# Two-layer attention and retention trunk: products of constants ahead of the first tokens, and a new order of the first loads and steps

## The chip, the core and the metric

The kernel runs on one core of a Trainium2 chip. A core has five engines, each with its own queue of instructions that it works through in order: TensorE (PE, matrix products and transposes; PEld is its loading of the stationary operand), VectorE (DVE), ScalarE (ACT), GpSimd (POOL) and SyncE (SP), which here only issues transfers. The transfers themselves are carried out by 16 DMA engines. The metric is the device time of one execution in microseconds (us); lower is better.

## The reference

The input is one sequence of 2048 tokens with 1024 features. Each of two layers normalises the tokens, projects them to eight sections of 512 columns, runs chunked softmax attention on one half of the heads and chunkwise retention on the other, gates both and adds the output projection:

```python
def hybrid_layer(x, norm_gain, w_in, w_out, rel_bias, cos, sin):
    hn = rms_norm(x, norm_gain)
    proj = hn @ w_in.astype(hn.dtype)
    aq, ak, av, ag, rq, rk, rv, rg = jnp.split(proj, cuts, axis=-1)
    ya = chunked_rel_attention(aq, ak, av, rel_bias)
    yr = chunkwise_retention(rq, rk, rv, cos, sin)
    y = jnp.concatenate([ya * jax.nn.silu(ag), yr * jax.nn.silu(rg)], axis=-1)
    return x + y @ w_out.astype(x.dtype)
```

The tables cos and sin come from the integer positions, times a fixed list of inverse frequencies. The result is normalised once more. All arithmetic of the reference is float32.

## The kernel before

Every float32 operand of a large product is split into an upper half (float16) and a lower half (the float16 rest), and a product is three products of halves: upper by upper, upper by lower, lower by upper. So a weight section passes through five steps before PE can use it: its squares are summed (ACT, L1346), the sum is cast (DVE, L1350) and added over the partitions by a product with ones (PE, L1356), a power-of-two scale is made of it by five small steps (DVE, L1363 to L1367), the upper half is written (ACT, L1426) and then the lower half (DVE, L1429). A token tile of 128 tokens has its own chain: squares (ACT, L249), root (DVE L210, POOL L212), scaling by root and gain (DVE, L256), eight transposes for each tile in the first group (PE, L265), upper half (ACT, L274) and lower half (DVE, L283).

The sweep goes over two layers, four weight groups s and four token groups n of 512 tokens (four tiles each). Before the first group can be multiplied, its four token tiles x0 to x3, four weight sections W0 to W3 (for q, k and the retention's q and k) and then four sections V0 to V3 have to be loaded and converted; tiles x4 to x7 of the next token group are loaded behind them. The first group's products come in this order on PE: sections 0 and 1 token tile by token tile (L722, 24 products of 128 columns for each pair of section and tile), sections 2 and 3 for all 512 tokens at once (L740, 24 products of 512 columns each), then the products with V (dense_V, L760, four tiles of 24 products). From then on PE has the work of all later groups.

The order of work on all engines is written out by hand. All first loads are issued on SP in one list (L1397, before any step). Then `do` runs a string of step names, and each step appends its instructions to the queues of the engines that it uses. The names that matter here:

- `xsq3 xrs3 xmul3 xtr3 xhi3 xlo3`: squares, root, scaling, transposes, upper and lower half of token tile 3; `xdma` is the transfer that transposes the halves of tiles 4 and up (SP, L236 and L237).
- `Wsq2 Wlp2 Wsc2 Whi2 Wlo2`: squares, cast, scale, upper and lower half of weight section 2; `V` for the V sections. W2 and W3, V0 and V1, V2 and V3 share their cast and scale.
- `g`: the next of three steps of the gain's own scale (DVE and PE, L165 to L189). Its input is the small load `gs`. `gb` is the load of the gain rows for all partitions, which `xmul` reads.
- `t`: the next step of the rotary tables (L89 to L125): the first in the string is the product of positions and inverse frequencies (ACT, L99, loads `pos` and `inv`), then come small reductions on DVE (L93 to L115) and sines on ACT. `u` is the same for two later groups.
- `r`: the relative bias (load `rl`): six transposes and a copy (L541, L542), then twelve products and two copies (L547, L548). `bs` and `bt` build bias tiles of it.
- `d`: the next part of the first group's products: eight parts of 24 products (L722), two evacuations, then three parts of eight (L740) and an evacuation for each of the sections 2 and 3.
- `Tu`, `Vu`: small scales that follow from the sections' scales; `Tu` also scales the retention's mask (load `msk`).

After the string, the generator dense_V and the dense products of the three following groups run in parts of eight products. With each part one pair of `ring["listed"]` is taken: the first of its two strings runs ahead of that part's attention work and the second behind it. This list of 96 pairs holds the steps of tiles 4 to 15 and those of the next weight group (`T` and `U` names).

`ms0` is a tile of 1024 float32 columns in PSUM; each weight scale uses two columns of its lower half. `ones` is a column of ones in bfloat16, set by POOL at the start and broadcast to a 128x128 operand.

Of the kernel before, what the change touches and what calls it, by code (L numbers as in the profile page):

```python
# [18 lines left out]
P = 128  # L19
# [8 lines left out]
def hybrid_trunk(ctx: ExitStack, tc: tile.TileContext, x, pos, gain, gcol, w_in, w_out, rel, fgain,  # L28
# [8 lines left out]
    act, dve, pool, pe, sp = nc.scalar, nc.vector, nc.gpsimd, nc.tensor, nc.sync  # L37
# [20 lines left out]
    ones = cp.tile([P, 1], BF16, tag="ones", name="ones")  # L58
# [24 lines left out]
    def tables(ns, wk):  # L83

        ang, k, r, k2 = wk
        pi = k2.bitcast(I32)
        for i, n in enumerate(ns):
            src = pos[n * 512:(n + 1) * 512].rearrange("(h c) -> h c", h=2)[None].to_broadcast([64, 2, 256])
            sp.dma_start(pi[:, i * 256:(i + 1) * 256], src)  # L89
        yield  # L90

        def mulsub(dst, kk, c):
            dve.scalar_tensor_tensor(out=dst, in0=kk, scalar=-c, in1=dst, op0=ALU.mult, op1=ALU.add)  # L93

        def rnd(dst, src, mul):
            dve.tensor_scalar(dst, src, mul, MAGIC, op0=ALU.mult, op1=ALU.add)
            dve.tensor_scalar(dst, dst, -MAGIC, None, op0=ALU.add)

        act.activation(ang, pi, AF.Copy, scale=invf_sb[:, 0:1])  # L99
        yield  # L100
        rnd(k, ang, 1.0 / P1)
        yield
        for c in (PA, PB, PC):
            mulsub(ang, k, c)
            yield
        dve.scalar_tensor_tensor(out=k2, in0=k, scalar=-(PD + PE_), in1=ang, op0=ALU.mult, op1=ALU.add)
        yield
        rnd(k2, k2, 1.0 / TWO_PI)
        yield
        for kk, c in ((k2, QA), (k, PD), (k2, QB), (k, PE_), (k2, QC)):  # L110
            mulsub(ang, kk, c)
            yield
        dve.tensor_scalar(ang, ang, PI_CL, -PI_CL, op0=ALU.min, op1=ALU.max)
        yield
        dve.scalar_tensor_tensor(out=k, in0=ang, scalar=-1.0, in1=ang, op0=ALU.mult, op1=ALU.max)  # L115
        yield
        act.activation(r, ang, AF.Sin)
        act.activation(k2, k, AF.Sin, scale=-1.0, bias=quarter[:, 0:1])
        yield
        act.activation(ang, r, AF.Copy, scale=-1.0)  # L120
        yield
        def store(i, n):
            for part, src in enumerate((k2, k2, ang, r)):
                rows = tab_d[n][part // 2, part % 2 * 64:part % 2 * 64 + 64].rearrange("f (h c) -> (f h) c", h=2)
                sp.dma_start(rows, src[:, i * 256:(i + 1) * 256])  # L125
            tab_done.add(n)

        store(0, ns[0])
        if len(ns) > 1:
            later(7, lambda: store(1, ns[1]))  # L130
        yield
# [69 lines left out]
    ring = {}  # L201
# [325 lines left out]
    def rel_reverse():  # L527

        c8 = (RELW + 1) // P
        rl = b2.tile([P, D], F32, tag="q", name="rl")  # L530
        rt = b1.tile([P, c8, NH], F32, tag="dT", name="rt")
        anti = b1.tile([P, KT, P], F16, tag="ktok", name="anti").rearrange("p k c -> p (k c)").bitcast(F32)[:, 0:P]
        pool.memset(rl[0:NH, 0:RELW + 1], 0.0)
        pool.memset(anti, 0.0)
        pool.affine_select(out=anti, in_=anti, compare_op=ALU.not_equal, fill=1.0, base=1 - P, pattern=[[1, P]],
                           channel_multiplier=1)
        sp.dma_start(rl[0:NH, 0:RELW], rel)
        yield
        ps = psR.tile([P, c8, NH], F32, tag="small", name="rlt")
        for c in range(c8):  # L540
            pe.transpose(ps[:, c, :], rl[0:NH, c * P:(c + 1) * P], ident[0:NH, 0:NH])  # L541
        dve.tensor_copy(rt, ps)  # L542
        yield
        for hf in range(2):
            pr = psR.tile([P, c8 // 2, P], F32, tag="small", name=f"rlr{hf}")
            for c in range(c8 // 2):
                pe.matmul(pr[0:NH, c, :], rt[:, c8 - 1 - hf * c8 // 2 - c, :], anti, start=True, stop=True)  # L547
            dve.tensor_copy(rl[0:NH, hf * P * c8 // 2:(hf + 1) * P * c8 // 2],  # L548
                            pr[0:NH].rearrange("p c i -> p (c i)"))
        sp.dma_start(rel_d, rl[0:NH, 0:RELW + 1])  # L550
        yield
# [45 lines left out]
    def later(k, fn):  # L597
        deferred.append([k, fn])
# [734 lines left out]
    def go_on(*gens):  # L1333
        for g_ in gens:
            next(g_, None)
# [40 lines left out]
    t0 = tables((0,), [gp.tile([P, 256], F32, tag="gt", name=f"wk{i}") for i in range(4)])  # L1376
    rl_ = rel_reverse()
# [15 lines left out]
    for j in range(4):  # L1393
        loads[f"V{j}"] = lambda j=j: v_in(j)
        if j < 3:
            loads[f"W{j}"] = lambda j=j: W.load(j)
    for nm in "x0 gs msk W0 gb x1 inv pos x2 W1 x3 rl W2 W3 dc V0 V1 V2 V3 x4 x5 x6 x7".split():  # L1397
        loads[nm]()
    gs = gain_scale(0)
    ms0 = psS.tile([P, D], F32, tag="S", name="ms0")  # L1400
    spare = [h_.rearrange("p k c -> p (k c)")[:, i * 2 * D:(i + 1) * 2 * D] for h_ in far[1] for i in range(2)]
    xk = [Tok(t, xs0[t], None) if t < 4 else Tok(t, late[t - 4], spare[t - 4]) for t in range(8)]
    d0 = dense_T(0, 0, 0, g00, st0)
# [37 lines left out]
    def V_un():  # L1441
        if not vu:
            vu.append(V_units(0, 0, g00, scs["V0"].i + scs["V2"].i, "V0_0"))
        next(vu[0])

    t1 = tables((1, 2), [xs0[1 + i // 2][:, i % 2 * 512:(i % 2 + 1) * 512] for i in range(4)])
    x8 = (sp.dma_start(late[t - 8], x[t * P:(t + 1) * P, :]) for t in range(8, 12))
    steps = {"x8": lambda: go_on(x8), "d": lambda: go_on(d0), "t": lambda: go_on(t0), "u": lambda: go_on(t1), "r": lambda: go_on(rl_), "g": lambda: go_on(gs),
             "Tu": T_un, "Vu": V_un, "bs": lambda: go_on(bs0), "bt": lambda: go_on(bt0)}
    for t in range(8):  # L1450
        for f in ("sq", "rs", "mul", "tr", "hi", "lo", "dma"):
# [7 lines left out]
    def do(names):  # L1459
        for nm in names.split():  # L1460
            steps[nm]()

    do("g xsq0 xrs0 Wsq0 xsq1 g Wlp0 g Wsc0 xmul0 Whi0 xtr0 xsq2 t xrs1 xhi0 xmul1 Wsq1 Wlo0 xrs2 t xtr1 xlo0 t Wlp1 "
# [3 lines left out]
    g00.vdone = 4  # L1467
    ring["listed"] = iter([("xrs5 u xrs6 xmul5 xhi4 bt", "xhi5 xmul6 xlo5"), ("", "xlo4"), ("xdma5", ""), ("bt", "bt xrs7 xhi6"),
# [16 lines left out]
    LAYER = [("", "yl0 yl1"), ("ys1", ""), ("", "xl0"), ("ys0", "yc0"), ("", "yh0"), ("", "yc1"), ("", ""),  # L1485
# [31 lines left out]
    for l in range(DEPTH):  # L1517
        gO = [Grp(), Grp()]
        go = Grp()
        for s in range(NSW):  # L1520
            g = grp(l, s)
            for n in range(NS):
# [7 lines left out]
                if n == 0 and not first:  # L1530
                    bs, bt = bias_scratch(l, s), bias_tiles(l, s, g)
# [116 lines left out]
```

## Time and profile before

| | before |
|---|---|
| runs, median of 3 | 2003.63 us (2002.98 to 2003.68) |
| the profiled execution | 2002.48 us |
| its span in the profile | 2000.6 us |
| PE busy from 0 to 50 us | 35.49 us |
| PE busy from 50 to 100 us | 49.59 us |
| PE busy from 100 to 150 us | 50.00 us |
| DMA moved from 0 to 50 us | 252 GB/s |

The span is the time from the first to the last recorded instruction; the profiled execution's own time is 1.9 us longer. In a row of a timeline the first number is the start in us from the span's start, the second the duration in us, then engine, source line, operation, the tile that is written, an arrow, the tiles that are read, shapes and count; a bracket at the end gives the idle time of that engine before the instruction and what ended it. Rows of one line that follow each other are merged, with their count behind an x; a merged row's duration reaches from the first start to the last end, and the end of a product includes the time in which its results drain. Tile names carry no numbers: `xa` holds x0 and x1, `xb` x2 and x3, `stT` W0 to W2, `wk` the positions and the tables, `ptn` the transposed tokens, `hTh` and `hTl` the tokens' halves, `whT` and `wlT` the weights'; parts of `hTh` and `hTl` that belong to later groups hold W3, the V sections and x4 to x7 in the meantime. In a row of a transfer the last number is the time from issue to landing in us.

### The profile page before, as it was taken

The numbers are of one execution on the slowest core, as the hardware profiler recorded it, in microseconds if no ns is written. First come the engines' busy times: TensorE is split into PE (matmuls) and PEld (weight loads), VectorE is DVE, ScalarE is ACT, GpSimd is POOL, SyncE is SP. The second block draws the span as 40 slices with busy tenths as digits, with TensorE's granted clock in tenths as the row PEclk, the third lists the DMA queues.
The fourth block names the chain that finished last, engine by engine and source line by source line (L and its number), as shares of the span: only waits on it lengthen the run. The fifth ranks groups of instructions, "written<-read, shape, count | busy, mean of one in ns | idle before, by whom it ended". The sixth has DMA issues, their size and how long they took to land.

```text
span 2000.6 us, 36774 instructions
## 1 busy us (share of the span) xinstructions
PE 1976.8 (99%) x12894; PEld 1042.5 (52%) x12894; DVE 1233.3 (62%) x3662; ACT 1155.6 (58%) x2526; POOL 701.2 (35%) x701
## 2 busy tenths in 40 slices
PE   7999999999999999999999999999999999999998
PEld 5455555555555555554445555555555555555544
DVE  8787756665556655677545556555655565567543
ACT  8667756465656545656345556565656565456432
POOL 1454433434434334420013444343444334343100
PEclk9999999999999999999999999999999999999999
DMA  8889755576565654999964457574847475558864
GB/s 252 206 179 196 173 118 140 136 145 133 131 139 133 142 126 117 194 249 278 235 165 97 115 114 162 117 153 106 168 116 164 98 169 126 120 126 189 234 204 133
DMA packets 651706, 315.05 MB, mean 157 GB/s; under 512 B 465248, under 2 KB 608096, under 8 KB 651520
## 3 DMA queue, kind: packets, MB, share of 16 engines
q1 hardware_dynamic: 651520, 312.70, 67.8%
q8 instruction: 101, 1.65, 0.3%
q14 instruction: 85, 0.70, 0.1%
HBM read 123.26 MB, written 41.98 MB: 83 GB/s over the span
## 4 chain that ended last, share of the span: by engine, by line
PE 94%; DMA 1%; SPq 1%; POOL 1%; DVE 1%; issue 1%; ACT 1%; POOLq 0%; ACTq 0%; DVEq 0%
PE dT L740 32%; PE dV L760 31%; PE dO L1106 16%; PE r L865 4%; PE o L830 3%; PE S L808 3%; PE S L809 3%; PE o L831 2%; DMA pT<-pq 1%; DMA swp<-rot 0%; SPq L820 0%; PE dT L722 0%; DMA rl<-in_rel_dram 0%; POOL pq L818 0%; SPq L1392 0%
## 5 line engine op out<-in xcount | busy, mean ns | idle before, releaser
L818 POOL TENSOR_TENSOR pq<-sc,pq 128x640 f16<-128x640 f32 (+4 forms) x256 | 324.1, 1266 | 947.6 <-ACT pq L817 464.8
L815 ACT ACTIVATE sc<-sc,mq,cT 128x640 f32<-128x640 f32 (+4 forms) x256 | 218.4, 853 | 402.0 <-DVE mq L814 290.3
L760 PE MATMUL dV<-wlV,hTh 128*128 128x512 f16 x1024 | 351.5, 379 | 0.0
L760 PE MATMUL dV<-whV,hTh 128*128 128x512 f16 x1024 | 351.5, 379 | 0.0
L760 PE MATMUL dV<-whV,hTl 128*128 128x512 f16 x1024 | 351.5, 379 | 0.0
L740 PE MATMUL dT<-hTh,whT 128*128 128x512 f16 x1008 | 346.6, 379 | 0.4 <-DVE hTl L279 0.4
L740 PE MATMUL dT<-hTh,wlT 128*128 128x512 f16 x1008 | 346.6, 379 | 0.0
L740 PE MATMUL dT<-hTl,whT 128*128 128x512 f16 x1008 | 346.6, 379 | 0.0
L760 PEld LDWEIGHTS <-hTh 128*128 128x128 f16 x2048 | 195.8, 98 | 211.6
L740 PEld LDWEIGHTS <-whT 128*128 128x128 f16 x2016 | 192.1, 98 | 205.7 <-DVE hTl L279 0.9
L812 DVE CUSTOM_DVE_ANT_0 sc<-S,bias 128x640 f32<-128x640 f32 (+4 forms) x256 | 188.9, 738 | 136.7 <-PE S L809 135.9
L1106 PE MATMUL dO<-wlO,yhy 128*128 128x512 f16 x504 | 191.0, 379 | 0.0
L1106 PE MATMUL dO<-whO,yhy 128*128 128x512 f16 x504 | 191.0, 379 | 0.0
L1106 PE MATMUL dO<-whO,yly 128*128 128x512 f16 x504 | 191.0, 379 | 0.0
L817 ACT ACTIVATE pq<-sc 128x640 f16<-128x640 f32 (+4 forms) x256 | 171.5, 670 | 8.1
L1106 PEld LDWEIGHTS <-yhy 128*128 128x128 f16 x1008 | 98.0, 98 | 113.2
L760 PEld LDWEIGHTS <-hTl 128*128 128x128 f16 x1024 | 98.9, 98 | 110.1
L740 PEld LDWEIGHTS <-wlT 128*128 128x128 f16 x1008 | 97.3, 98 | 108.1
L808 PE MATMUL S<-k,q 128*128 128x128 f16 (+3 forms) x592 | 142.4, 267 | 0.0
L830 PE MATMUL o<-v,pT 128*128 128x129 f16 x1120 | 132.4, 221 | 2.0 <-DMA pT<-pq 1.8
L809 PE MATMUL S<-k,q 128*128 128x128 f16 (+3 forms) x592 | 129.3, 266 | 0.0
L831 PE MATMUL o<-v,pT 128*128 128x65 f16 x1120 | 125.7, 193 | 0.0
(358 smaller groups left out, 3252.0 us busy)
## 6 DMA issues: line engine op xcount, KB each, us to landing
q<-qq SPq DMA_DIRECT2D x128, 128.0 KB, 2.4
yyy<-y_d SPq DMA_DIRECT2D x32, 512.0 KB, 4.4
stT<-in_w_in_dram SPq DMA_DIRECT2D x27, 512.0 KB, 5.0
stV<-in_w_in_dram SPq DMA_DIRECT2D x26, 512.0 KB, 4.7
k<-kk SPq DMA_DIRECT2D x128, 64.0 KB, 2.0
swp<-rot SPq DMA_DIRECT2D x64, 128.0 KB, 3.0
tabc<-tab SPq DMA_DIRECT2D x32, 256.0 KB, 2.9
tabs<-tab SPq DMA_DIRECT2D x32, 256.0 KB, 3.1
```

Source lines behind the costliest of these rows:

```text
L740: pe.matmul(ps, w_[:, j, kt, :], h_[:, kt, :], start=(m == 0), stop=(m == 23))
L760: pe.matmul(ps, h_[:, kt, a * P:(a + 1) * P], w_[:, kt, :], start=(m == 0), stop=(m == 23))
L808: pe.matmul(o, st.q[:, hx, 0, cs], k_, start=True, stop=False)
L809: pe.matmul(o, st.q[:, hx, 1, cs], k_, start=False, stop=True)
L812: dve.tensor_tensor_reduce(out=v, in0=S[:, 0:w], in1=g.bias[hx][:, 640 - w:640], scale=1.0, scalar=-3.0e38, op0=ALU.add, op1=ALU.max, accu ...
L815: act.activation(v, v, AF.Exp, bias=m[:, 0:1], scale=g.c[:, 0:1])
L817: act.activation(pq[:, 0:w], v, AF.Copy)
L818: pool.tensor_tensor(pq[:, w:2 * w], v, pq[:, 0:w], op=ALU.subtract)
L830: pe.matmul(o[:, u.hx, 0:129], u.p[:, b, :], v_, start=(b == 0), stop=False)
L831: pe.matmul(o[:, u.hx, 0:65], u.p[:, u.nb + b, :], v_[:, 0:65], start=False, stop=(b == u.nb - 1))
L865: pe.matmul(out_, w_, m_, start=(i == 0), stop=(i + 1 == len(pairs)))
L1106: pe.matmul(ps, h_[:, kt, :], w_[:, kt, :], start=(m == 0), stop=(m == 23))
```

## The change

Four things change: the list of first loads has a new order, a step `w` is new that puts two products of ones by ones (128 stationary columns, 512 moving columns) on PE with the unused half of `ms0` as output, the step string of the first group has a new order with fourteen `w` in it, and the list of pairs behind it has a new order. The set of all other steps is the same.

```diff
-    for nm in "x0 gs msk W0 gb x1 inv pos x2 W1 x3 rl W2 W3 dc V0 V1 V2 V3 x4 x5 x6 x7".split():
+    for nm in "gs x0 W0 x1 gb x2 x3 inv pos W1 W2 V3 W3 dc V1 rl msk V0 x5 V2 x7 x4 x6".split():
...
+    def warm():
+        for _ in range(2):
+            pe.matmul(ms0[:, 512:1024], ones.to_broadcast([P, P]), ones.to_broadcast([P, 512]), start=True, stop=True)
+
...
-    do("g xsq0 xrs0 Wsq0 xsq1 g Wlp0 g Wsc0 xmul0 Whi0 xtr0 xsq2 t xrs1 xhi0 xmul1 Wsq1 Wlo0 xrs2 t xtr1 xlo0 t Wlp1 "
-       "xmul2 xsq3 xrs3 t d xhi1 Wsc1 t Whi1 xtr2 xlo1 t Wsq2 xmul3 xhi2 Wsq3 xlo2 Wlp2 r d t xtr3 Vsq0 Wlo1 Wsc2 xhi3 "
-       "d Vsq1 Whi2 Whi3 Vlp0 xlo3 d t Vsc0 d Vsq3 d Wlo2 Vsq2 r Vlp2 t Wlo3 t d Tu u Vhi1 t d d t bs xsq4 d Vhi0 t "
-       "xrs4 Vsc2 t xsq7 d Vhi3 Vhi2 Vu t d t xsq6 xmul4 t xsq5 d Vlo1 Vlo3 d d Vu d Vlo2 Vlo0 d d")
+    do("w w g w xsq0 Wsq0 g w xrs0 w g Wlp0 w Wsc0 w w w xsq1 Whi0 xmul0 xtr0 xsq2 w w xrs1 xmul1 xtr1 t xrs2 xhi0 "
+       "Wsq1 xsq3 w Wlo0 t xlo0 xhi1 xmul2 Wlp1 t d xrs3 w Wsc1 xtr2 Wsq2 xhi2 xlo1 xmul3 Whi1 xlo2 d t Wsq3 Wlp2 w "
+       "xtr3 d t Wlo1 r Vsq3 Vsq1 t Wsc2 t r Vsq0 Vlp0 t xhi3 Tu Whi3 xlo3 bs Whi2 t Wlo3 d d t d Vsc0 d Vsq2 t Vlp2 "
+       "Wlo2 xsq4 d xrs4 u Vhi0 Vsc2 t d d Vhi1 d Vhi2 Vu t xsq7 Vlo0 t Vhi3 t d t d Vu xmul4 t Vlo2 Vlo3 xsq6 xsq5 d "
+       "d d d d Vlo1")
...
-    ring["listed"] = iter([("xrs5 u xrs6 xmul5 xhi4 bt", "xhi5 xmul6 xlo5"), ("", "xlo4"), ("xdma5", ""), ("bt", "bt xrs7 xhi6"),
-                   ("u u", "xmul7 xlo6"), ("u", ""), ("", ""), ("bt", "xdma4"), ("xhi7 x8 u", "u xdma6"), ("", "xlo7 u"),
-                   ("xdma7", "x8"), ("", "x8"), ("u", "u"), ("xin10 xin9", "u u"), ("u", "x8 u"), ("u u", "u"), ("u", ""),
...
+    ring["listed"] = iter([("xhi4 xrs5 xrs6 xmul5", "xmul6 xhi5 xlo5 xlo4"), ("xhi6", ""), ("u bt", "xlo6"), ("xrs7 u", "u"),
+                   ("bt xmul7 xdma5", ""), ("", "xdma4 xhi7 u u"), ("", ""), ("", ""), ("xdma6 u bt", ""),
+                   ("xlo7 xdma7 u", ""), ("x8", ""), ("", "u x8 bt"), ("u u", "u"), ("", "u x8 u xin9"),
...
```

The entries of the list that are left out here move by at most six pairs, most of them by two or less.

More of the change, by code (lines that the diff above doesn't have):

```diff
@@ L1444, in V_un @@
         next(vu[0])
+    def warm():
+        for _ in range(2):
+            pe.matmul(ms0[:, 512:1024], ones.to_broadcast([P, P]), ones.to_broadcast([P, 512]), start=True, stop=True)
     t1 = tables((1, 2), [xs0[1 + i // 2][:, i % 2 * 512:(i % 2 + 1) * 512] for i in range(4)])
     x8 = (sp.dma_start(late[t - 8], x[t * P:(t + 1) * P, :]) for t in range(8, 12))
-    steps = {"x8": lambda: go_on(x8), "d": lambda: go_on(d0), "t": lambda: go_on(t0), "u": lambda: go_on(t1), "r": lambda: go_on(rl_), "g": lambda: go_on(gs),
+    steps = {"x8": lambda: go_on(x8), "d": lambda: go_on(d0), "t": lambda: go_on(t0), "u": lambda: go_on(t1), "r": lambda: go_on(rl_), "g": lambda: go_on(gs), "w": warm,
              "Tu": T_un, "Vu": V_un, "bs": lambda: go_on(bs0), "bt": lambda: go_on(bt0)}
```

28 rows, old and new, of the table steps are left out of this document.

## The prediction

> **What bounds the kernel now.** I read the page first, then busy time by stretches, then the timeline of the first 70 us engine by engine, and last the transfers with their time from issue to landing.
>
> ```profile
> span 2000.6 us, 36774 instructions
> PE 1976.8 (99%) x12894; PEld 1042.5 (52%) x12894; DVE 1233.3 (62%) x3662; ACT 1155.6 (58%) x2526; POOL 701.2 (35%) x701
> ```
>
> TensorE (PE) is busy for 1976.8 of 2000.6 us, so it sets the end: a change gains only what it takes out of PE's 23.8 us of idle time, or out of matmuls that run slowly. The rows of two stretches (length, then busy time of PE, PEld, DVE, ACT, POOL, with counts; granted clock, DMA share, GB/s) say where that is.
>
> ```profile
> 12.60:36.00 23.40, 20.97 (x251) 18.50 (x252) 21.99 (x55) 22.05 (x41) 1.80 (x3) 1.00 0.93 278
> 36.00:2000.60 1964.60, 1955.33 (x12642) 1023.62 (x12640) 1206.17 (x3576) 1128.15 (x2478) 696.92 (x685) 1.00 0.68 155
> ```
>
> After 36 us PE lacks 9.3 us in all; before it, 14.5 us (23.8 less 9.3), and the change edits that part. Between 12.6 and 36 us VectorE (DVE) is busy for 21.99 and ScalarE (ACT) for 22.05 of 23.4 us: there PE waits for two full engines, not the reverse.
>
> **The change part by part.** (a) The fill. Fourteen steps "w" put 28 products of 512 columns on PE, nine of the steps ahead of the first token's transposes.
>
> ```profile
> 12.57 3.98 PE L265 MATMUL ptn<-ident,xa 128*128 128x128 f32 x16 [3.13 <-DVE xa L256]
> 16.36 1.16 PE L722 MATMUL dT<-hTh,whT 128*128 128x128 f16 x8
> 17.31 0.88 PE L722 MATMUL dT<-hTl,whT 128*128 128x128 f16 x8
> 18.02 0.61 PE L722 MATMUL dT<-hTh,wlT 128*128 128x128 f16 x8
> 19.48 1.07 PE L265 MATMUL ptn<-ident,xb 128*128 128x128 f32 x8 [0.84 <-DVE ssn L210]
> ```
>
> The first 16 transposes fill 12.57 to 16.36, 0.237 us each; later 8 take 1.07 us with their tail of 0.27, about 0.114 each. The first 8 products of 128 columns take 0.95 us up to the next row, 0.119 each; the third 8 end within 0.61, about 0.056 each. So PE runs at half its speed up to about 17.4 us, although the granted clock reads 1.00 throughout. At full speed the 16 transposes save 16 x 0.123 = 1.97 us and the first 24 products 2.11 - 24 x 0.056 = 0.77: 2.74 us of PE time. A product of 512 columns is four of 128: 0.22 to 0.48 us, so the 18 ahead of the transposes take 4.0 to 8.6 us, and the last six of them, between the first weight scale and the first transposes, 1.3 to 2.9. They cost nothing as long as they end before the first token is scaled, at 11.7 (below): the weight sum that precedes them ends at 8.9, so even the slow six end at 11.8. The later five steps stand in PE waits for tokens. The saving is nothing too if what follows the transposes is late for another reason; (c) shows that it is.
>
> [...]
>
> (b) The loads. All go down one queue. Landing is issue plus lag, or the end of an ACT wait.
>
> ```profile
> 7.89 1.06 ACT L1346 ACTIVATE whT<-stT 128x1024 f16<-128x1024 f32 x1 [2.58 <-DMA stT<-in_w_in_dram]
> 10.95 1.06 ACT L249 ACTIVATE hTh<-xa 128x1024 f16<-128x1024 f32 x1 [1.91 <-DMA xa<-in_x_dram]
> 14.18 1.06 ACT L249 ACTIVATE hTh<-xb 128x1024 f16<-128x1024 f32 x1 [1.04 <-DMA xb<-in_x_dram]
> 2.60 0.58 SPq L156 DMA_DIRECT2D gb<-in_gain_dram  x1
> gb<-in_gain_dram SPq DMA_DIRECT2D x1, 512.0 KB, 7.1
> 4.43 1.37 SPq L89 DMA_DIRECT2D wk<-in_pos_dram  x1
> wk<-in_pos_dram SPq DMA_DIRECT2D x1, 128.0 KB, 8.4
> 6.53 0.53 SPq L298 DMA_DIRECT2D stT<-in_w_in_dram  x1
> stT<-in_w_in_dram SPq DMA_DIRECT2D x1, 512.0 KB, 9.5
> 7.10 2.55 SPq L1392 DMA_DIRECT2D xb<-in_x_dram  x1
> xb<-in_x_dram SPq DMA_DIRECT2D x1, 512.0 KB, 10.3
> ```
>
> So W0 lands at 7.85, the gain rows gb at 9.7, x1 at 10.9, the positions at 12.8, x2 at 14.15, W1 at 16.0, x3 at 17.4: in the order of issue. The steps are 1.85 for gb and W1, 1.3 for a token tile (x1 1.2, x3 1.4), and 3.2 for x2 with the positions, so 1.9 for positions and inverse frequencies. In the new order, with the mask no longer ahead: W0 7.4, x1 9.0, gb 10.4, x2 11.8, x3 13.1, positions 14.9, W1 16.7. Tokens come 2 to 4 us earlier; positions 2.1 and W1 0.7 us later. Behind them each W or V takes 1.8, which puts the relative bias (rl) at 24.1 and V0 at 26.1, just ahead of their first uses.
>
> (c) The steps of the first group, each time from the row named.
>
> ```profile
> 9.07 0.16 DVE L1350 CAST mbW<-m1W 128x1 bf16<-128x1 f32 x1 [1.94 <-ACT whT L1346]
> 9.14 0.15 DVE L329 TENSOR_SCALAR m2h<-msh 128x1 f32<-128x1 f32 x1
> 10.47 0.15 DVE L1363 TENSOR_SCALAR sc0W<-ms 128x1 f32<-128x1 f32 x1
> 11.23 1.28 DVE L256 SCALAR_TENSOR_TENSOR xa<-xa,rsn,gb 128x1024 f32<-128x1024 f32 x1
> 15.24 0.49 ACT L99 ACTIVATE wk<-wk,invf_sb 128x256 f32<-128x256 int32 x1
> 15.64 1.24 ACT L274 ACTIVATE hTh<-ptn,gv 128x512 f16<-128x512 f32 x2
> 15.77 0.29 DVE L96 TENSOR_SCALAR wk<-wk 128x256 f32<-128x256 f32 x1
> 30.44 1.28 DVE L1429 SCALAR_TENSOR_TENSOR wlT<-stT,sc2W,whT 128x1024 f16<-128x1024 f32 x1
> 31.80 1.20 DVE L548 COPY rl<-rlr 16x384 f32<-16x384 f32 x2
> 32.99 0.41 DVE L93 SCALAR_TENSOR_TENSOR wk<-wk,wk 128x256 f32<-128x256 f32 x1
> 33.33 1.27 DVE L1429 SCALAR_TENSOR_TENSOR wlT<-hTh,sc2W,whT 128x1024 f16<-128x1024 f32 x1
> 34.52 0.40 DVE L93 SCALAR_TENSOR_TENSOR wk<-wk,wk 128x256 f32<-128x256 f32 x1
> 35.07 0.38 PE L740 MATMUL dT<-hTh,whT 128*128 128x512 f16 x1
> 45.42 1.89 PE L760 MATMUL dV<-whV,hTh 128*128 128x512 f16 x8
> ```
>
> Now the third gain step (9.14 to 10.47, 1.33 us) stands on DVE behind the cast for W0; the new order runs it in the wait for W0. W0 at 7.4, its squares 1.2 us later, cast at 8.6, the sum on PE, five scale steps of 0.76 from 9.1: DVE could scale the first token at 9.9, but gb lands at 10.4. It starts at 10.4 instead of 11.23 and ends at 11.7. The second follows at 12.4 (the 0.7 us root on POOL between them stays) and W0's rest at 13.8.
>
> On ACT, though, the angle step (L99) stands ahead of the first token's upper half (L274), and needs the positions: 14.9 instead of 15.24. Behind it wait all of ACT's steps, W1's squares among them. DVE's reduction (L96) comes at 15.4, not 15.77: 0.35 us ahead, and this is all the lead. The first products start at 16.5 with the clock up or not, since slow transposes, too, are done by 13.7: that wait is the cover of (a).
>
> From L96 on DVE is full, so I count what stands ahead of Wlo2, the lower half of the third weight section, which PE needs for its first wide products (35.07). Before, it starts at 30.44. The new order puts ahead of it the lower half of the fourth section, 1.2 us (33.33 to 34.52), both bias copies, 1.13 (31.80 to 32.93), three table steps of 0.34 (32.99 to 33.33), the mask set-up and one cast, about 0.6: 3.95 us. DVE waits 0.3 us more, for W3's squares. Wlo2 starts at 30.44 - 0.35 + 3.95 + 0.3 = 34.35 and ends at 35.6. The first wide product does not read it, the second does, so the wide products start 0.2 earlier, at 35.4: 0.35 us later than before, 0.4 with the handover. PE's own work would have let them start at 34.6. Here the early tokens' gain ends.
>
> (d) What follows: the wide products fill 35.07 to 45.42, then come the products with V.
>
> ```profile
> 38.32 2.19 ACT L1426 ACTIVATE whV<-hTl,sc2V 128x1024 f16<-128x1024 f32 x2
> 63.38 1.23 SPq L236 DMA_TRANSPOSE hTh<-hTl  x1
> hTh<-hTl SPq DMA_TRANSPOSE x1, 3.2
> 65.93 0.38 PE L760 MATMUL dV<-wlV,hTh 128*128 128x512 f16 x1
> 66.72 1.89 PE L740 MATMUL dT<-hTh,whT 128*128 128x512 f16 x8 [0.41 <-DVE hTl L279]
> 174.97 0.23 PE L830 MATMUL o<-v,pT 128*128 128x129 f16 x1 [1.02 <-DMA pT<-pq]
> ```
>
> V's last upper half now ends at 40.5, 4.9 us before its use; the new order, which puts one behind the tables, keeps about 3. At 66 PE waits: its last V product is issued at 65.93, the next would follow 0.22 later, but starts at 66.72, 0.57 late. The profile names DVE; the transpose of the last token's upper half, issued at 63.38 and landed 3.2 later at 66.58, fits better. That half (xhi7) moves from the ninth pair of the list to the sixth, at 1.7 us a pair (twelve from 45.42 to 66.15) some 4 us earlier, and its transpose moves before xlo7's end: the 0.57 us go. The other entries move mostly by two pairs or less; I cost them at nothing, since PE lacks only 9.3 us after 36 and waits there for little but the rows above; the bounds are -1.0, the wait at 175 gone, and +1.7, one transpose a pair late.
>
> The sum: +0.4 - 0.57 = -0.2 us. The profiled execution took 2002.48 (span 2000.6 and 1.9 around it), the median of three is 2003.63; on the median this gives 2003.5.
>
> **Rivals.** (1) The start gains as meant: the positions and W1 land no later than before, so DVE's waits of 0.5 (gb), 0.5 (positions) and 0.3 (W3's squares) go. Wlo2 ends 1.3 us earlier, the gap at 66 and that at 175 (1.02) close: -0.9 - 0.57 - 1.02 = -2.5, 2001.1. For it: small transfers might overtake; against it: every row above lands in order. Even with 1 us more it stops at 2000, since DVE's work stays.
> [...]
> (2) Slower: ACT's queue stands behind the positions. From 14.9 on, each us that they are late delays the first upper half, DVE's reduction and Wlo2 by one. x3's issue was held for 2.55 us, and x3 landed at 17.4; positions issued behind such a hold could land there: +2.5, so 2003.5 + 2.5 = 2006.0. For it: rl and V0, 0.7 and 0.2 us ahead of their uses, would be late as well. Against it: the bytes ahead of them have shrunk by the mask, and the queue was full already.
> (3) The fill doesn't raise the clock, or it falls again between 6.5 and 8.8 us: the first products take 0.77 us longer, but wait for W0's rest anyway; at most +0.8, 2004.3.
> (4) Later list entries miss by three pairs of 1.7 us: +5.1, 2008.6. Against it: most move by less. PE's idle time after 180 us would show it.
>
> **How the numbers follow.** Forecast, no change, 2003.5, with a range of its own of 2002.2 to 2004.9: 0.60. Rival 1: 0.16; 2: 0.14; 3: 0.05; 4: 0.05. A measurement tells 0.2%, 4.0 us, from no change. Faster than 1999.6 needs more than rival 1 and DVE's work leave: 0.04. Slower than 2007.6 has a part of rival 2 and most of 4: 0.08. The rest is 0.88. Leaving out a tenth on each side, the range ends at 2000.8 (rival 1 with a little more) and 2006.3 (rival 2).
>
> **What would show it.** Right: first transposes at about 11.8 us, 0.12 us each; first products at 16 to 17 all the same; an ACT wait for positions (13 to 15 us) at L99; PE waiting about 1 us for Wlo2 (L1429) ahead of the first L740, which starts near 35.4; no wait at 66; the same rows after 180 us. Wrong: L740 before 34 (the loads or DVE were not the bound) or after 37 (they bind harder), transposes at 0.24 us, or new PE waits after 70 us.

## The result

The changed kernel is slower: 2008.3 us as the median of 22 runs (2003.0 to 2015.5) against 2003.28 of the kernel before in the same session (22 runs, 2001.46 to 2004.4). The ratio is 1.0024, with a 95% interval of 1.0017 to 1.0031. Forecast were 2003.5 us and a range from 2000.8 to 2006.3. Two things were not expected: the 5 us, and that the runs of one kernel now lie 12.5 us apart instead of 2.9.

The profiled execution of the changed kernel took 2005.38 us, one of its quicker ones, and 2.90 more than the profiled one of before (2002.48). So this trace holds about three of the five microseconds; where an execution near the median loses the rest, no trace of this kernel shows. Two lines of its page:

```profile
span 2003.6 us, 36837 instructions
PE 1986.3 (99%) x12921; PEld 1044.7 (52%) x12922; DVE 1233.6 (62%) x3662; ACT 1156.1 (58%) x2526; POOL 703.6 (35%) x701
```

The two stretches of the prediction again (length, then busy time of PE, PEld, DVE, ACT and POOL with counts, granted clock, DMA share, GB/s):

```profile
12.60:36.00 23.40, 21.91 (x257) 18.15 (x257) 21.81 (x61) 21.31 (x39) 2.86 (x4) 0.91 0.97 275
36.00:2003.60 1967.60, 1955.75 (x12641) 1022.88 (x12639) 1205.81 (x3570) 1127.65 (x2477) 697.70 (x683) 1.00 0.68 155
```

PE is busy 9.5 us more than before, nearly all of it ahead of 36 us, where the fill is. After 36 us it has the same work as before (1955.75 against 1955.33 us of busy time), but lacks 11.85 us where it lacked 9.27: of the 3.0 us by which the span grew, 2.6 are waits after 36 us. At the start nothing was lost. PE's rows there (start, duration) are these:

```profile
11.28 1.11 PE L265 MATMUL ptn<-ident,xa 128*128 128x128 f32 x4 [0.77 <-DVE ssn L210]
13.04 1.91 PE L1448 MATMUL ms<-ones 128*128 128x512 bf16 x4
17.12 0.61 PE L722 MATMUL dT<-hTh,whT 128*128 128x128 f16 x8
34.26 0.38 PE L740 MATMUL dT<-hTh,whT 128*128 128x512 f16 x1
35.05 0.39 PE L740 MATMUL dT<-hTh,wlT 128*128 128x512 f16 x1 [0.41 <-DVE wlT L1429]
65.92 1.89 PE L740 MATMUL dT<-hTh,whT 128*128 128x512 f16 x8
```

The second wide product runs at 35.05; before, the second was at 35.28, one product behind the first at 35.07. So PE has 0.2 us of lead from here on, and the wait at 66 us is gone (more on it under (d) below). The loss must come later. Here are PE's waits over the whole span (who waits and for whom: us in all, times, longest), first before the change, then after it:

```profile
PE o L830 <- DMA pT<-pq: 1.8, 2, 1.0
PE r L865 <- DVE dT L873: 0.3, 1, 0.3
```

```profile
PE o L830 <- DMA pT<-pq: 4.1, 5, 1.2
PE r L865 <- DVE dT L873: 0.9, 1, 0.9
```

L830 is the attention's product with V. It reads pT, which a transposing DMA (L820, on SP's queue) makes of the probabilities. The other row, 0.6 us more in one wait at 1818 us, was not followed further. Two of the new waits of L830 on PE, and the transpose of the first of them on SP's queue:

```profile
458.81 0.23 PE L830 MATMUL o<-v,pT 128*128 128x129 f16 x1 [1.18 <-DMA pT<-pq]
1827.79 0.23 PE L830 MATMUL o<-v,pT 128*128 128x129 f16 x1 [1.10 <-DMA pT<-pq]
```

```profile
452.28 3.22 SPq L820 DMA_TRANSPOSE pT<-pq  x1
```

The 3.22 us are the time on SP's queue; this transpose lands at 458.76, 6.48 us after its issue. The DMA engines in the stretch from 452.2 to 458.8 us, by queue (packets, MB, and the sum of the packets' times as a share of 16 engines; it goes over 100% because packets of one engine overlap):

```profile
q1 hardware_dynamic: 2564, 1.11, 116.1%
q8 instruction: 1, 0.02, 0.8%
q14 instruction: 1, 0.01, 0.3%
```

Besides the kernel's own transfers there are two packets of instructions. The page says how many q8 brings in all (101 before the change, too):

```profile
q8 instruction: 101, 1.65, 0.4%
```

That is 101 packets of 16 KB (1.65 MB / 101). PE and PEld together have 12,921 + 12,922 = 25,843 records, 256 for each packet; and from one packet to the next PE works through 256 to 258 records in the median. So by these counts this queue brings PE's own instructions, in blocks of 256; a kernel with 256 more has 102 packets (e6_tiny128, below). In the packets' times the first comes at 27.0 us before the change and at 23.7 after it, and the median step is 19.1 us in both. The wait at 458.81 has the fetch of 453.62 in the flight of its transpose (the time from issue to landing). In the kernel before, the corresponding transpose is issued at 451.98, lands 4.73 us later and is used at 457.16; the fetch comes at 458.04, behind the use. The fill's 28 products with their 28 weight loads are 56 instructions, 56 / 256 of a block, so each later border falls 56 / 256 x 19.1 = 4.2 us of PE's work earlier (an estimate).

### The profile page after: what moved, and what is told of

It reads as the page before. It is cut to its first block, busy times and chain, and to the rows that moved or that the text cites. A ratio compares the mean times of both kernels' runs of the same rounds, so it can differ in the third digit from the quotient of the medians.

```text
span 2003.6 us, 36837 instructions
## 1 busy us (share of the span) xinstructions
PE 1986.3 (99%) x12921; PEld 1044.7 (52%) x12922; DVE 1233.6 (62%) x3662; ACT 1156.1 (58%) x2526; POOL 703.6 (35%) x701
## 3 DMA queue, kind: packets, MB, share of 16 engines
q8 instruction: 101, 1.65, 0.4%
## 4 chain that ended last, share of the span: by engine, by line
PE 53%; DVE 1%; POOL 1%; ACT 1%; DMA 1%; issue 0%; SPq 0%; POOLq 0%; ACTq 0%
PE dT L740 16%; PE dV L760 16%; PE dO L1106 14%; PE r L865 2%; PE o L830 2%; PE S L808 1%; PE S L809 1%; PE o L831 1%; DMA pT<-pq 0%; DMA yly<-hTh 0%; DMA swp<-rot 0%; DVE sc L812 0%; ACT sc L815 0%; PE ptn L1011 0%; POOL swp L681 0%
## 5 line engine op out<-in xcount | busy, mean ns | idle before, releaser
L740 PE MATMUL dT<-hTh,wlT 128*128 128x512 f16 x1008 | 346.6, 379 | 0.4 <-DVE wlT L1429 0.4
L740 PE MATMUL dT<-hTl,whT 128*128 128x512 f16 x1008 | 346.6, 379 | 0.0
L740 PE MATMUL dT<-hTh,whT 128*128 128x512 f16 x1008 | 346.6, 379 | 0.0
L740 PEld LDWEIGHTS <-whT 128*128 128x128 f16 x2016 | 192.1, 98 | 205.1
L740 PEld LDWEIGHTS <-wlT 128*128 128x128 f16 x1008 | 97.2, 98 | 108.8 <-DVE wlT L1429 0.7
L830 PE MATMUL o<-v,pT 128*128 128x129 f16 x1120 | 132.5, 221 | 4.1 <-DMA pT<-pq 4.1
```

Of the source, the lines that this page charges most:

```text
L740: pe.matmul(ps, w_[:, j, kt, :], h_[:, kt, :], start=(m == 0), stop=(m == 23))
L830: pe.matmul(o[:, u.hx, 0:129], u.p[:, b, :], v_, start=(b == 0), stop=False)
```

## The experiments

Three theories were set against each other. The list theory: the moved entries of the later list put transposes late. The fetch theory: the fill shifts PE's instruction blocks against its work, and fetches now meet transposes. The start theory: the small lead of PE leaves the transposes less time. The order of instructions explains little here: on SP, ACT, DVE and POOL the same work comes in the same order as before from about 265 us on, while new waits come until 1828 us. All times are medians, with their ratio to the kernel before on the same chip and its 95% interval.

**The fill taken away (e1_no_fill).**

```diff
-    do("w w g w xsq0 Wsq0 g w xrs0 w g Wlp0 w Wsc0 w w w xsq1 Whi0 xmul0 xtr0 xsq2 w w xrs1 xmul1 xtr1 t xrs2 xhi0 "
+    do("g xsq0 Wsq0 g xrs0 g Wlp0 Wsc0 xsq1 Whi0 xmul0 xtr0 xsq2 xrs1 xmul1 xtr1 t xrs2 xhi0 "
...
```

> The changed kernel without its 28 products of constants; new load order, new steps and new list stay. List theory (the moved entries of the list change the order of the queue of transfers up to some 400 us, so transposes of P land late): still about 2008, spread of 10 us or more. Fill theory (the 28 products put 56 instructions more ahead of all of TensorE's later ones, so the blocks of 16 KB in which its instructions are fetched, every 18.5 us, come 4 us earlier against the work and now run into transposes of P): back near 2003.3, spread of 3 us. Start theory (TensorE 0.25 us ahead of before from 36 us on leaves the transposes less lead): still about 2008 if the start keeps that lead.

Measured: 2003.63 us (11 runs, 2002.31 to 2004.94), ratio 0.9999 (0.9991 to 1.0008). The whole loss goes with the fill, and the spread with it. So the new loads, steps and list together cost nothing and bring nothing that can be told (the interval is about 1.7 us to either side); the start theory falls with it, since this kernel's second wide product runs at 34.50, more ahead than the changed one's.

**The old list (e2_old_list).** The 96 pairs of before stand in the changed kernel.

```diff
-    ring["listed"] = iter([("xhi4 xrs5 xrs6 xmul5", "xmul6 xhi5 xlo5 xlo4"), ("xhi6", ""), ("u bt", "xlo6"), ("xrs7 u", "u"),
+    ring["listed"] = iter([("xrs5 u xrs6 xmul5 xhi4 bt", "xhi5 xmul6 xlo5"), ("", "xlo4"), ("xdma5", ""), ("bt", "bt xrs7 xhi6"),
...
```

> The changed kernel with the list of before (the steps of later groups back in their old places); fill, loads and first steps stay new. List theory: back to 2003 to 2004, with the wait of 0.6 us at 66 us. Fill theory: still 2007 to 2009, wide spread. Start theory: still 2007 to 2009.

Measured: 2008.8 us (8 runs), ratio 1.0026 (1.0016 to 1.0036). The loss stays: the list is not its cause.

**The fill alone (e3_fill_alone).** Fourteen steps "w" of two products among the old steps.

```diff
-    do("g xsq0 xrs0 Wsq0 xsq1 g Wlp0 g Wsc0 xmul0 Whi0 xtr0 xsq2 t xrs1 xhi0 xmul1 Wsq1 Wlo0 xrs2 t xtr1 xlo0 t Wlp1 "
+    do("w w g w xsq0 xrs0 w w Wsq0 xsq1 g w Wlp0 g w Wsc0 w w w xmul0 Whi0 xtr0 w w w w xsq2 t xrs1 xhi0 xmul1 Wsq1 Wlo0 xrs2 t xtr1 xlo0 t Wlp1 "
...
```

> The kernel before with the 28 products alone, put among its old steps in TensorE's waits of the first 20 us; loads, steps and list are those of before. Fill theory: 2007 to 2009, wide spread. List theory and start theory: 2003.3 within 1 us, spread of 3 us.

Measured: 2008.34 us (12 runs, 2005.05 to 2012.65), ratio 1.0023 (1.0015 to 1.0032), though its first wide product starts at 35.12 as before. The fill by itself makes the loss. Its worst wait, from PE's rows and then in stretches of 1 us (columns as above):

```profile
174.68 0.38 PE L740 MATMUL dT<-hTh,wlT 128*128 128x512 f16 x1
178.47 0.23 PE L830 MATMUL o<-v,pT 128*128 128x129 f16 x1 [3.41 <-DMA pT<-pq]
180.04 0.63 PE L740 MATMUL dT<-hTl,whT 128*128 128x512 f16 x1
180.47 0.63 PE L740 MATMUL dT<-hTh,whT 128*128 128x512 f16 x1
182.44 0.38 PE L740 MATMUL dT<-hTl,whT 128*128 128x512 f16 x1
```

```profile
173.50:174.50 1.00, 1.00 (x7) 0.42 (x5) 1.00 (x1) 1.00 (x3) 1.00 (x2) 1.00 1.21 126
174.50:175.50 1.00, 0.56 (x3) 0.07 (x1) 1.00 (x5) 1.00 (x4) 0.53 (x1) 1.00 2.70 169
175.50:176.50 1.00, 0.00 (x0) 0.00 (x0) 0.38 (x3) 0.90 (x2) 0.00 (x0) 1.00 0.18 29
176.50:177.50 1.00, 0.00 (x0) 0.00 (x0) 0.09 (x1) 0.00 (x0) 0.00 (x0) 1.00 1.31 117
177.50:178.50 1.00, 0.03 (x1) 0.03 (x2) 0.00 (x0) 0.00 (x0) 0.00 (x0) 1.00 1.26 296
```

```profile
q14 instruction: 1, 0.01, 5.5%
q8 instruction: 1, 0.02, 3.1%
```

The transpose was issued at 171.77 and landed at 178.42, 6.65 us later; before the change the corresponding one took 5.36 (169.56 to 174.93) and PE waited 1.02. So of the 2.4 us that PE waits longer, 1.3 are the longer flight. The other 1.1 are a late issue: SP's queue is 2.2 us behind the kernel before, PE's own work only 1.1. This begins 35 us earlier: two transfers for the rotation (swp), issued at 135.76 and 136.28, take 6.7 us instead of 4.8, with the fetch of 138.72 in their flights (in the kernel before it came at 140.73, when they had all but landed). POOL's step L680, which waits for them, starts at 143.15 instead of 141.08, and SP's queue, which waits for POOL's later steps, goes on at 148.06 instead of 145.26. So one late landing held back others behind it here.

Between 174.5 and 176.5 us (last fence, by queue) both instruction queues fetch, and in the second half of that time all transfers together fall to 29 GB/s while transposes are waited for. Behind the wait, PE takes 0.425 us from one wide product to the next at 180 us instead of 0.213. So the clock was lower there for a while (last section). Against the kernel before, PE is 1.1 us late ahead of this wait, 3.5 behind it (178.47 for 174.97) and 5.1 when it is back at full speed (the wide product at 182.17 stood at 177.05): this one wait, with the clock behind it, makes 4 of the 6.7 us by which this execution is longer (2009.18 against 2002.48).

**The list alone (e4_list_alone).** The kernel before with the new list, as in the change's diff.

> The kernel before with the new list alone; no fill, old loads and old first steps. List theory: 2007 to 2009, wide spread. Fill theory: 2003.3, or 0.6 us less where the wait at 66 us goes. Start theory: 2003.3.

Measured: 2003.38 us (11 runs), ratio 1.0000 (0.9991 to 1.0008). No difference can be told.

**The same instructions with hardly any work (e5_tiny28).** The fill could act by its instructions or by its work. So the 28 products keep their places and shrink to one column by one row:

```diff
+    def warm():
+        for _ in range(2):
+            pe.matmul(ms0[0:1, 512:513], ones, ones, start=True, stop=True)
```

> The kernel before with 28 products of one column by one row in place of those of 512 columns, at the same places: 56 TensorE instructions more, but hardly any work. Fetch theory (what counts is where the borders of the 256-instruction blocks of 16 KB fall): 2007 to 2010, wide spread, long waits for transposes of P with a fetch in them, as with the fill alone. Clock theory (the fill's work changes the granted clock, and that costs): 2003.5 within 1 us, spread of 4 us.

Measured: 2007.7 us (11 runs, 2006.03 to 2010.61), ratio 1.0021 (1.0012 to 1.0030). The instructions do it, not their work; the clock theory falls.

**A whole block (e6_tiny128).** As before, with 16 steps of 8 in the first 12 us: 256 instructions.

```diff
+        for _ in range(8):
...
+    do("w w w w w g w w w w xsq0 xrs0 w Wsq0 xsq1 g w w w w Wlp0 g w Wsc0 w xmul0 Whi0 xtr0 xsq2 t xrs1 xhi0 xmul1 Wsq1 Wlo0 xrs2 t xtr1 xlo0 t Wlp1 "
```

> The kernel before with 128 such products of one column by one row in TensorE's first idle time: 256 instructions, one whole block, so every later border falls on the same instruction as before. Fetch theory: 2003.3 to 2004.5 with the spread of before, though 100 more are added than in the kernel with 28. Any theory by which added products cost time in proportion, or by which their mere presence does: 2008 or more.

Measured: 2003.71 us (11 runs, 2002.3 to 2004.96), ratio 1.0000 (0.9991 to 1.0009). This is the run that decides: 4.6 times as many products, and the loss is gone. Its page shows one fetch more, and its waits for pT are 1.2 us where the 28 made 4.3 (first the 28, then the 128):

```profile
PE o L830 <- DMA pT<-pq: 4.3, 5, 2.5
q8 instruction: 101, 1.65, 0.4%
```

```profile
PE o L830 <- DMA pT<-pq: 1.2, 2, 1.0
q8 instruction: 102, 1.67, 0.4%
```

**The changed kernel, filled up to a block (e7_after128).** Fill, loads, steps and list stay; 100 small products are added in ten steps "k", each a call of more().

```diff
+    def more():
+        for _ in range(10):
+            pe.matmul(ms0[0:1, 512:513], ones, ones, start=True, stop=True)
...
-    do("w w g w xsq0 Wsq0 g w xrs0 w g Wlp0 w Wsc0 w w w xsq1 Whi0 xmul0 xtr0 xsq2 w w xrs1 xmul1 xtr1 t xrs2 xhi0 "
+    do("w w g w xsq0 Wsq0 g w xrs0 w k k k k g Wlp0 w k Wsc0 w w w xsq1 Whi0 xmul0 xtr0 xsq2 w w k k xrs1 xmul1 xtr1 t xrs2 xhi0 "
```

> The changed kernel with its fill, loads, steps and list as they are, and 100 products of one column by one row besides, so that 256 instructions are added in all: one whole block. Fetch theory: the 5 us of loss go, 2002.5 to 2004.5 (up to 1 us of it for products that do not fit into TensorE's waits). Other theories: 2008 or more.

Measured: 2003.9 us (11 runs, 2001.92 to 2006.51), ratio 1.0004 (0.9995 to 1.0013). Work added to the changed kernel makes it 4 us faster, which is as fast as the kernel before.

**Other shifts (e8_tiny64, e9_tiny14, e10_tiny96, e11_tiny112).** The kernel before with 4, 1, 6 or 7 small products in each step (14 steps for the 14, else 16).

> The kernel before with 64 products of one column by one row: 128 instructions, half a block, so fetches come some 9 us earlier against the work. Fetch theory gives no sign here, only that the time goes by which transposes the fetches meet: anything from 2001 to 2010, with waits for transposes at other places than before. Other theories: 2003.3, or between the kernels with 28 and 128 products.

> The kernel before with 14 products of one column by one row: 28 instructions, fetches 2.0 us earlier against the work. An estimate by the fetch theory, from the trace of before: a transpose of P with a 16 KB fetch in its flight lands 1.1 to 1.5 us later than one without (4.07 against 2.97 there, 4.48 against 2.96 after the change), say 1.2; moving every fetch of that trace 2.0 us earlier and adding 1.2 to the transposes that are newly met, TensorE waits 2.8 to 3.4 us more (1.2 of it at 175 us, 0.7 to 0.8 each at 457, 813 and 1825): 2006.5 to 2007.1. A cost in proportion to the number of products would give half of that of 28, 2005.8.

> The kernel before with 96 such products: 192 instructions, fetches 4.6 us later against the work. The same estimate gives 1.7 to 2.2 us: 2005.4 to 2005.9, with no new wait at 175 us.

> The kernel before with 112 such products: 224 instructions, fetches 2.3 us later against the work. The same estimate gives -0.3 to 1.1 us: 2003.4 to 2004.8, so hardly to be told from before, though four times as many products as in the change are added.

| small products | shift of the fetches | estimate | median | ratio (95%) |
|---|---|---|---|---|
| 14 | 28 instructions earlier | 2006.5 to 2007.1 | 2005.33 | 1.0009 (1.0000 to 1.0018) |
| 28 | 56 earlier | 2007 to 2010 | 2007.70 | 1.0021 (1.0012 to 1.0030) |
| 64 | 128, half a block | no sign | 2005.89 | 1.0014 (1.0005 to 1.0023) |
| 96 | 64 later | 2005.4 to 2005.9 | 2004.53 | 1.0009 (1.0000 to 1.0018) |
| 112 | 32 later | 2003.4 to 2004.8 | 2004.16 | 1.0003 (0.9994 to 1.0011) |
| 128 | none | 2003.3 to 2004.5 | 2003.71 | 1.0000 (0.9991 to 1.0009) |

The loss goes with the place in the block, not with the number of products: 28 and 64 cost time, 128 do not. The rows of 14, 96 and 112 alone can't be told from no change; their intervals reach 1.0000 or below. The 64 wait at other places than the 28: of PE's waits for DMA in that kernel the largest are

```profile
PE dO L1106 <- DMA yhy<-hTh: 1.2, 1, 1.2
PE dT L740 <- DMA hTl<-hTl: 0.9, 1, 0.9
PE dT L740 <- DMA hTl<-xa: 0.7, 1, 0.7
PE o L830 <- DMA pT<-pq: 0.6, 1, 0.6
```

so other transposes, of the normalised tokens and of the gated results, are the ones that come late there. The medians of 112, 96 and 14 have the order of the estimates, but 14 and 96 lie below theirs: 14 made 1.8 us instead of 3, 96 made 1.0 instead of 1.7 to 2.2. For the 14 the rival, a cost in proportion to the number of products, was nearer with 2005.8; it fails for 64, 96, 112 and 128. The places were missed, too. The estimate had 1.2 us more for the 14 at 175 us and new waits at 457, 813 and 1825; in the profiled execution the wait at 175 is 1.26 us, where it was 1.02, and the others are not there; for the 96 it had no new wait at 175 us, and the wait there is 1.78 us, where it was 1.02. So the estimate from single transposes did not work, and the theory rests on 28, 128 and the changed kernel filled up to a block.

One reason for the size: I took 1.1 to 1.5 us for a fetch from all flights with and without one, and a long flight is likelier to contain a fetch. Comparing the same transpose of pT behind 400 us in the traces before and after the change: where a fetch starts between 1 us ahead of the issue and 3 us behind it in only one of the two kernels, that flight is 0.70 us longer (49 such after the change, 41 before it); where neither has one, the difference is 0.03 (110). This is the direct sign that a fetch delays a transpose. With 0.7 in the same estimate the 28 would make only about 1.4 us, and 2.5 with the fetches counted as in this comparison, not 4. The kernel with the fill alone shows two things that the estimate leaves out, the queue that a late landing holds back and the lower clock behind a long wait; how much they make in the other kernels stays open. The single flights vary much more than the mean (2.3 to 8.2 us before the change).

How a fetch delays a transpose can be followed one step further in the packets. These stretches are full of packets of 256 bytes that take 18 ns in the median. Some take over 1.2 us, and these come in groups that end together: behind 60 us there are 41 such groups before the change and 46 after it. Of them 27 and 28 end 1 to 4 us behind the start of a 16 KB fetch, of which there are 98 in that time; spread by chance over 19.1 us it would be 3 / 19.1 of the groups, 6 to 7. So about one fetch in four is followed by a stall of the DMA engines' small packets. Why only one in four, and what they wait for, the records don't show.

## Why the prediction was wrong, point by point

**(a) The fill: here the sum failed.** The time of its first part was sized and hidden as said: the 18 products up to the first transposes took 2.74 + 1.87 + 1.01 + 1.62 = 7.2 us (forecast 4.0 to 8.6) and ended at 10.5:

```profile
0.93 2.74 PE L1448 MATMUL ms<-ones 128*128 128x512 bf16 x6 [0.93 <-POOL ones L59]
3.53 1.87 PE L1448 MATMUL ms<-ones 128*128 128x512 bf16 x4
5.54 1.01 PE L1448 MATMUL ms<-ones 128*128 128x512 bf16 x2
8.89 1.62 PE L1448 MATMUL ms<-ones 128*128 128x512 bf16 x6 [0.25 <-DVE sc0W L1363]
```

The step that failed is "They cost nothing as long as they end before the first token is scaled". It priced an added instruction by its time alone. What it cost is a shift of PE's instruction stream against its work, a term that the sum doesn't have: +4.0 us for 56 instructions with next to no work (2007.70 against 2003.67), and nothing for 256 (2003.71). Also "The later five steps stand in PE waits for tokens" was wrong in part: six of their products, slow as they are, run from 13.04 and from 16.46 with no wait of PE behind them, and the first products start at 17.12 (forecast 16.5), without the fill (e1_no_fill) at 15.07; the second wide product comes at 35.05 against 34.50. That half microsecond can't be told in the time.

**The clock** (rival 3) fell again, as that rival said, though later than it said. In stretches of the changed kernel:

```profile
0.00:10.00 10.00, 6.78 (x21) 2.36 (x21) 4.05 (x31) 5.41 (x9) 2.48 (x13) 1.00 0.82 264
10.00:17.00 7.00, 6.23 (x24) 4.29 (x23) 6.30 (x10) 4.46 (x9) 2.23 (x2) 0.51 1.00 287
```

The first six products of the fill run about 0.47 us apart, although the granted clock reads 1.00 in that stretch; the last six ahead of the tokens 0.25, near the 0.213 of full speed. But from 10 to 17 us the granted clock is 0.51, and the transposes run at half speed as before (8 in 1.91 us). PE had stood still from 6.55 to 8.48; that this wait is the reason isn't shown. So the fill saved nothing for the transposes. That products ahead of them bring them to full speed was the author's estimate; the first eight take 1.97 us here and 1.85 with the fill alone, where later ones took 1.07 before the change. The first products with weights (L722) do run at full speed (8 in 0.61), but they start at 17.12, when they have waited for the slow part of the fill.

**(b) The loads** came in the order of issue, but 0.5 to 1.7 us earlier than forecast:

```profile
9.94 1.28 DVE L256 SCALAR_TENSOR_TENSOR xa<-xa,rsn,gb 128x1024 f32<-128x1024 f32 x1 [0.42 <-DMA gb<-in_gain_dram]
11.06 1.06 ACT L249 ACTIVATE hTh<-xb 128x1024 f16<-128x1024 f32 x1 [0.50 <-DMA xb<-in_x_dram]
13.26 0.51 ACT L99 ACTIVATE wk<-wk,invf_sb 128x256 f32<-128x256 int32 x1 [1.05 <-DMA wk<-in_pos_dram]
15.91 1.06 ACT L1346 ACTIVATE whT<-stT 128x1024 f16<-128x1024 f32 x1 [0.98 <-DMA stT<-in_w_in_dram]
```

So the gain rows landed at 9.9 (forecast 10.4), x2 at 11.05 (11.8), the positions at 13.2 (14.9) and W1 at 15.9 (16.7). Rival 2, positions that are late, is out.

**(c) The steps.** The binding waits were named rightly: gb for the first scaling, the positions for ACT, Wlo2 for the wide products. The lead of the loads went through to L96 and was eaten by the steps put ahead of Wlo2, as said, all 0.6 to 1.0 us earlier than the numbers:

```profile
14.42 0.29 DVE L96 TENSOR_SCALAR wk<-wk 128x256 f32<-128x256 f32 x1
33.71 1.28 DVE L1429 SCALAR_TENSOR_TENSOR wlT<-stT,sc2W,whT 128x1024 f16<-128x1024 f32 x1
```

L96 at 14.42 for 15.4, Wlo2 at 33.71 for 34.35. So the wide products were 0.2 us earlier, not 0.4 later.

**(d) What follows.** The wait at 66 us went, but by luck. The transpose was issued at 60.49, 2.9 us earlier than before (forecast about 4), but its flight, taken over as 3.2 us, grew to 5.1, so it landed only 1.1 us earlier:

```profile
hTh<-hTl SPq DMA_TRANSPOSE x1, 5.1
```

In e1_no_fill and e4_list_alone, with the same new list, it takes 5.6 and 5.8 us, and PE waits longer than the 0.57 us that were to be saved (rows in this order):

```profile
66.24 1.89 PE L740 MATMUL dT<-hTh,whT 128*128 128x512 f16 x8 [0.70 <-DVE xb L97]
67.46 1.24 PE L740 MATMUL dT<-hTh,whT 128*128 128x512 f16 x5 [0.92 <-DVE rot L688]
```

So the term of -0.57 us in the sum was wrong, too, by less than the times can tell. The list entries costed at nothing (one of them, Ulo1, moves by seven pairs) cost nothing that can be told (e4_list_alone). Rival 4 had the right sign, time (2008.6) and mark, idle time of PE after 180 us, but the wrong cause, so its number is luck: e2_old_list keeps the loss with the old list. Without the fill, the forecast of no change is what was measured (e1_no_fill, 2003.63).

## What to carry to other kernels

Before a few instructions are added to or taken from PE's stream, count them against 256 (the other engines were not tried): a change of microseconds with a wide spread, far behind the edit and on instructions that it doesn't touch, may be nothing but shifted instruction fetches. Test it by filling up to a whole block with products that do next to no work; if the loss goes, the edit itself was harmless. Transposes that land less than about 1 us ahead of their use (an estimate from the 0.70 us above) are where it can show, so they are what to mend: 18 of the 256 of pT in the kernel before, among them those used at 175, 457, 813, 878 and 1825 us.

## What the runs showed of the hardware

A block of 256 of PE's instructions comes as one packet of 16 KB in a queue (q8) that the page counts on the same 16 DMA engines as the kernel's transfers; the packet takes 1.0 us in the median before the change and 1.1 after it, and the next one comes 19.1 us later in the median. A transpose of pT that has such a fetch near its start lands 0.70 us later in the mean than the same one without (90 pairs).

A long wait of PE cost twice in two kernels. After the wait of 3.41 us in the kernel with the fill alone, the clock was granted at half for 3.4 us: the stretch behind it reads 0.66 in the mean, and five wide products of L740 took 0.425 us each instead of 0.213, 1.1 us more (1.6 with the others in that time).

```profile
178.00:183.00 5.00, 4.53 (x24) 2.24 (x25) 2.26 (x8) 1.51 (x2) 0.00 (x0) 0.66 0.82 189
183.00:190.00 7.00, 7.00 (x58) 3.91 (x55) 4.77 (x19) 3.29 (x8) 1.40 (x1) 1.00 0.43 99
```

The kernel with the old list (e2_old_list) shows the same behind a wait of 3.13 us that ended at 176.73:

```profile
176.00:181.00 5.00, 4.27 (x22) 2.22 (x23) 2.15 (x8) 1.08 (x2) 0.00 (x0) 0.66 0.88 204
```

At the start of the changed kernel the clock fell at 10.07 us, to half for 6.8 us, with no wait longer than 1.93 us in the fill; behind the waits of up to 1.2 us that came later it stayed up (1.00 from 16.90 to 2000.04). In the 3.41 us ahead of each fall, a stretch as long as the first of these waits, PE was busy for 0.38 us (fill alone, 175.44 to 178.85), 0.28 (old list, 173.49 to 176.90) and 1.34 (changed kernel, 6.66 to 10.07). Whether a wait makes the clock fall, and from what length on, these runs don't show.
